# TensorE's queue in program order through the first part of a two-block kernel, with the lanes' products interleaved by hand

## The chip, the cores and the metric

One Trainium2 chip, one of its cores. The metric is device time in microseconds (us) of one execution. Engines: TensorE (PE; its weight loads are PEld), VectorE (DVE), ScalarE (ACT), GpSimd (POOL), SyncE (SP). "q" behind an engine's name is its queue of DMA issues.

## What is computed

All in float32, 256 tokens of width 1024. The first block takes x through two attention layers and a final norm. The second block takes that x (256 tokens) and a context ctx (256 tokens) through two layers. A layer normalises both with a modulation from a conditioning vector, forms q, k, v, pool, convolution and gate projections, attends, merges three branches, and then applies a feed-forward part with 16384 experts of which each token chooses 16 in each of 8 heads:

```python
q = (xc @ w_q).reshape(PEER_CHUNK, PEER_HEADS, 2, PEER_HALF)
s = jnp.einsum('thid,hikd->thik', q, sub_keys)
s1, i1 = lax.top_k(s[:, :, 0], PEER_TOPK); s2, i2 = lax.top_k(s[:, :, 1], PEER_TOPK)
...
top_s, pos = lax.top_k(cand, PEER_TOPK)
gate = jax.nn.softmax(top_s, axis=-1)
hid = jax.nn.gelu(jnp.einsum('td,thkd->thk', xc, u_emb[eidx]))
return jnp.einsum('thk,thkd->td', gate * hid, v_emb[eidx])
```

In the last layer only x goes on; ctx gives keys and values.

## The kernel before

**Products.** A weight chunk is 128 x 1024 (512 KB). `WS` (L253) loads chunks on a DMA queue and splits each into a high part (ScalarE, L281) and a rest (VectorE, L282), `LEAD` = 2 chunks ahead; `mm3` (L405, L409 to L411) makes 24 matmuls of a chunk, three for each of 8 pieces. A chunk that is not split ("whole") goes through `mm1` (L416): 8 products in whole precision, each recorded as two matmuls. All SBUF tiles of 4 KB a partition share one pool of 42 pages ("pg"): chunks, splits, activations, gathered rows, tables. PSUM has 3 banks for products ("u") and 5 for all small work ("m").

**Who sets the order.** The program is a set of Python generators that record instructions; `lead`, `par` and `along` interleave them by the costs that they yield ("units"). `lead(main, (side, r))` advances the side until it has r units for each unit of the main lane; `par` advances whichever has the least share of its own weight; `along(main, side, rate)` takes one step of the side for each 1/rate units. The order in which the generators record is the program order. The context runs with a timeline simulation: each engine's queue is then filled by a scheduler that takes, at each moment of its simulated time, the first instruction in program order that is ready. On the chip each queue runs in the order so fixed.

**Stages.** (1) The x lane: the first block (`b1`, L693) and then layer 0's mixer for x. Beside it, at rate 2.0, the ctx lane: ctx's mixer, then ctx's choice of experts (`choose`) with layer 1's modulation. ctx's 256 tokens x 128 experts are computed by row operations (`rows`): each gathers one 128 x 1024 tile through POOL's queue (L1381) and takes one VectorE instruction (L1392, a dot product, or L1401, an accumulation). They start when ctx's lane is done, 0.32 for each unit of x's lane. (2) Layer 0's choice for x (`ffn_start`): `topk` makes 16 whole chunks of products and, for each head, four key scores (L1241) in one "m" bank, from which VectorE selects (L1248 to L1253); after heads 3 and 7 it combines (to L1309). The first `SOLO` = 24 steps run alone. Then `gbuild`: for 8 blocks of 32 tokens and 4 parts each, VectorE makes two one-hot operands (L1487, L1489), TensorE multiplies them (L1495), ScalarE evicts (L1499), and ScalarE's queue stores a block as 4 DMAs to a table G in DRAM (L1504). Beside it, at weights 100 and 20 x 3.41, `peer` makes the hidden products of the first 20 of 128 expert chunks, 16 of them whole. (3) The dense product (`peer`): for each of 128 expert chunks, the hidden product if not made yet, its weighting by G (loaded at L1548, L1551 to L1554) and 12 matmuls of 512 columns into four accumulators (L1578 to L1580). Row operations run along at 0.25 (choice) and 0.45 (dense product) for each unit. (4) Layer 1: mixer, choice, dense product.

**The norm.** `rms_bcast` (L464): squares on ScalarE (L472), a matmul with ones (L474), an eviction (L476), a second matmul (L479), thirteen small VectorE steps (L396 to L403), two diagonals (L498), and a matmul that spreads them over the partitions (L501). Before, nothing is yielded inside. `attn_causal` and `attn2` run a head in three steps: scores and softmax (`first`), transposes (`second`, one unit behind; L656, L1015), the product with v (`third`).

Of the kernel before, what the change touches and what calls it, by code (L numbers as in the profile page):

```python
# [34 lines left out]
NPRE = (16, 20), (20, 28)  # L35
# [257 lines left out]
class Ker:  # L293
# [170 lines left out]
    def rms_bcast(s, hch, n):  # L464

        nc = s.nc
        st = s.ps("m")
        if n == 8:

            for g in range(0, n, 4):  # L470
                sq = s.pg([128, 4, T], F32, "sq")
                nc.scalar.activation(sq, hch(g, 4), AF.Square)  # L472
                for k in range(4):
                    nc.tensor.matmul(st[32 * k:32 * k + 32, :T], s.ones[:, 0:32], sq[:, k], start=g == 0, stop=g == 4)  # L474
            gs = s.s1([128, T], "gs")
            nc.scalar.copy(gs, st[:, :T])  # L476
            ss = s.ps("m")
# [4 lines left out]
        else:  # L482
            for g in range(0, n, 4):
                m = min(4, n - g)
                sq = s.pg([128, 4, T], F32, "sq")
                nc.scalar.activation(sq[:, :m], hch(g, m), AF.Square)
                for k in range(m):
# [16 lines left out]
    def rms(s, h, n=8):  # L504
        rbs = s.s1([128, T], "rbs")
        s.nc.vector.tensor_copy(rbs, s.rms_bcast(lambda g, m: h.t[g // 4][:, :], n))
        return rbs

    def norm_hl(s, h, a, b, name, n=8, rbs=None):

        nc = s.nc
        rbs = rbs if rbs is not None else s.rms(h, n)
        o = HL(s, name, n)
        for k in range(n):
# [6 lines left out]
            else:  # L521
                nc.scalar.activation(oh, y, AF.Identity, bias=b(k))
                nc.vector.scalar_tensor_tensor(ol, y, b(k), oh, op0=OP.add, op1=OP.subtract)
        return o

    def norm_f(s, h, a, b, o):

        nc = s.nc
        rbs = s.rms(h)
        for k in range(8):  # L530
            y = s.s1([128, T], "ny")
            nc.vector.scalar_tensor_tensor(y, h.ch(k), a(k), rbs, op0=OP.mult, op1=OP.mult)
            nc.scalar.activation(o.ch(k), y, AF.Identity, bias=b(k))  # L533
        return o
# [88 lines left out]
    def attn_causal(s, scores, bias, init, scale, val, emit):  # L623
# [49 lines left out]
        for i in range(18):  # L673
            if i < 16:
                first(i)
            if 1 <= i < 17:
                second(i - 1)
            if i >= 2 and i % 2 == 1:
                third((i - 3) // 2)
            yield 1.7  # L680
# [12 lines left out]
    def b1(s, x, eng, out):  # L693
# [8 lines left out]
        hn = s.norm_hl(x, lambda k: s.V("norm_w", k), None, "hn")  # L702
        del x
        ws.load(W1)
        yield 1.0
# [81 lines left out]
        hn = s.norm_hl(x, lambda k: s.V("norm_w", 8 + k), None, "hn")  # L787
# [48 lines left out]
        cqn = s.norm_hl(cq, lambda k: s.V("cqn", k), None, "cqn", 2)  # L836
        ckn = s.norm_hl(ckv, lambda k: s.V("ckvn", k), None, "ckn", 1)
# [49 lines left out]
        rb = s.rms_bcast(lambda g, m: x.t[g // 4][:, :], 8)  # L887
# [7 lines left out]
    def rows_hl(s, rr, lo, n):  # L895
# [12 lines left out]
        nc.vector.tensor_tensor(rl[z], tb[z, :T], rh[z], op=OP.subtract)  # L908
        return rh[z], rl[z]


    def qkv(s, l, hn, ws, rope, want_q, r):
# [26 lines left out]
        for a, off, _ in todo:  # L939
            for hf in range(2):  # L940
                sq = s.pg([128, 4, T], F32, "sq")
                nc.scalar.activation(sq, a.t[hf], AF.Square)
                for k in range(4):
# [9 lines left out]
        rh, rl = s.rows_hl(rr, 0, 16)  # L953
        yield 8.0
# [29 lines left out]
    def attn2(s, l, q, kv, sr, o):  # L984
# [45 lines left out]
        for i in range(18):  # L1030
            if i < 16:
                first(i)
            if 1 <= i < 17:
                second(i - 1)
            if i >= 2:
                third(i - 2)
            yield 3.0

        bank = s.ps("m")
        for hf in range(2):  # L1040
            sq = s.pg([128, 4, T], F32, "sq")
            nc.scalar.activation(sq, o.t[hf], AF.Square)
            for k in range(4):
# [6 lines left out]
        rh, rl = s.rows_hl(rr, 64, 8)  # L1050
        yield 4.0
# [108 lines left out]
    def mixer(s, l, st, src, ws, eng, res, kvx, late=None, before=None, seq=False, h=None, rbs=None, side=None):  # L1160
# [7 lines left out]
        hn = s.norm_hl(h, lambda k: s.a1[l][:, k, st:st + 1], m0, "hn", rbs=rbs)  # L1168
# [50 lines left out]
        res["xn"] = s.norm_f(h, lambda k: s.a2[l][:, k, st:st + 1], s.mod(l, st, 3), Act(s, F32, "xn"))  # L1219
# [3 lines left out]
    def topk(s, l, xn, ws, eng, res, rows=False):  # L1223
# [8 lines left out]
        for h, sb in s.lin(ws, xn, 16):  # L1232
            if sb is None:
                yield 2.6
                continue
            qf = s.s2([128, 512], "qf")
            nc.scalar.copy(qf, sb)
# [17 lines left out]
            if h % 4 < 3:  # L1255
                continue
# [38 lines left out]
            for j in range(2):  # L1295
                for hf in range(2):
# [13 lines left out]
                    yield TY  # L1310
        ts = tp[:, 2].rearrange("p h t k -> p (h t) k")
# [158 lines left out]
    def gbuild(s, res, G, eng, ntc=8):  # L1470
# [7 lines left out]
        iob = io[:, None, :, :].to_broadcast(sh)  # L1478
# [289 lines left out]
```

## Time and profile before

| | us |
|---|---|
| median of 3 runs | 3698.21 |
| lowest, highest | 3693.96, 3700.71 |
| the profiled execution | 3691.09 |
| its span, first to last instruction | 3689.3 |
| busy in the span: PE, PEld, DVE | 3258.1, 2966.9, 2790.7 |
| ACT, POOL | 1485.0, 935.6 |
| moved by DMA | 941.10 MB, mean 255 GB/s |

A timeline row gives start, length, engine, line, operation, output <- inputs, count, and in brackets the idle time of the engine before it with what ended it. A wait row gives the waiting engine and line, the releaser, and the total, the number and the longest of the waits. A granted clock of 1.00 is TensorE's upper level (2.4 GHz), 0.50 the lower (1.2 GHz); in between is a mean over the stretch.

### The profile page before, as it was taken

Reading aid. Unit: us, or ns where it says so; the run is one execution under the profiler, and the core shown is the slowest. Engines: PE = TensorE matmul, PEld = TensorE weight load, DVE = VectorE, ACT = ScalarE, POOL = GpSimd, SP = SyncE. Lnnn points to the kernel's source line nnn. Section 1 sums busy time; section 2 is a strip of 40 time slices with the busy share of each in tenths; the row PEclk is TensorE's granted clock in tenths of the full one; section 3 lists DMA queues with packets and bytes.
Section 4 is the critical chain, followed back from the end, with each engine's and each line's share of the span. In section 5 each row is a group of like instructions: output and inputs, shape, how many; then the busy total and the mean of one; then the engine's idle time right before and its main releaser. Section 6 shows DMA issues by size and latency. Waiting matters only on the chain. (4 is left out here: it accounts for less than half of the span.)

```text
span 3689.3 us, 61049 instructions
## 1 busy us (share of the span) xinstructions
PE 3258.1 (88%) x23324; PEld 2966.9 (80%) x23324; DVE 2790.7 (76%) x5722; ACT 1485.0 (40%) x2785; POOL 935.6 (25%) x831
## 2 busy tenths in 40 slices
PE   6989989996799885679999999778998689999999
PEld 5976889766689774668888888767988589999999
DVE  4356585578899889799989999788465978777655
ACT  3444345323355313333443444333353154444443
POOL 2002101212343512365555555232000003111000
PEclk9989999998899897889999999888999899999999
DMA  8536446756688845999999999776525089888764
GB/s 298 160 126 215 146 138 189 274 183 225 238 299 280 321 161 181 344 408 386 384 379 386 379 387 381 248 280 231 158 88 192 12 262 354 307 285 286 263 217 153
DMA packets 315430, 941.10 MB, mean 255 GB/s; under 512 B 29616, under 2 KB 93136, under 8 KB 315136
## 3 DMA queue, kind: packets, MB, share of 16 engines
q1 hardware_dynamic: 130848, 468.77, 35.7%
q0 software_dynamic: 118816, 432.76, 32.3%
q10 hardware_dynamic: 65472, 35.66, 3.2%
q8 instruction: 183, 3.00, 0.3%
q14 instruction: 111, 0.91, 0.1%
HBM read 893.01 MB, written 43.02 MB: 254 GB/s over the span
## 5 line engine op out<-in xcount | busy, mean ns | idle before, releaser
L282 DVE TENSOR_TENSOR wb<-wr,wa 128x1024 fp32r<-128x1024 f32 x846 | 1015.4, 1222 | 321.5 <-ACT wa L281 304.9
L281 ACT CAST wa<-wr 128x1024 fp32r<-128x1024 f32 x846 | 856.3, 1046 | 108.3 <-DMA wr<-in_w 39.0
L409 PE MATMUL pu<-hnh,wa 128*128 128x256 f32 x2000 | 586.0, 293 | 47.9 <-ACT wa L281 45.9
L411 PE MATMUL pu<-hnh,wb 128*128 128x256 f32 x2000 | 583.4, 293 | 17.1 <-DVE wb L282 17.0
L410 PE MATMUL pu<-hnl,wa 128*128 128x256 f32 x2000 | 578.5, 290 | 0.0
L409 PE MATMUL pu<-xh,wa 128*128 128x256 f32 (+1 forms) x1760 | 492.1, 280 | 10.1 <-ACT wa L281 9.6
L1381 POOL DMA_INDIRECT row<-in_pu,ridx x256 | 365.1, 1426 | 520.7 <-DVE wb L282 124.5
L410 PE MATMUL pu<-xl,wa 128*128 128x256 f32 (+1 forms) x1760 | 491.2, 279 | 0.9 <-DVE xl L1538 0.9
L411 PE MATMUL pu<-xh,wb 128*128 128x256 f32 (+1 forms) x1760 | 491.4, 279 | 0.0
L1381 POOL DMA_INDIRECT row<-in_pv,ridx x256 | 354.4, 1384 | 473.5 <-DVE wb L282 133.0
L409 PEld LDWEIGHTS pu<-hnh,wa 128*128 128x128 f32 x2000 | 397.7, 199 | 65.0 <-ACT wa L281 52.0
L411 PEld LDWEIGHTS pu<-hnh,wb 128*128 128x128 f32 x2000 | 395.8, 198 | 32.5 <-DVE wb L282 21.9
L410 PEld LDWEIGHTS pu<-hnl,wa 128*128 128x128 f32 x2000 | 397.4, 199 | 3.9 <-issue 3.5
L409 PEld LDWEIGHTS pu<-xh,wa 128*128 128x128 f32 x1760 | 338.5, 192 | 20.1 <-ACT wa L281 14.5
L410 PEld LDWEIGHTS pu<-xl,wa 128*128 128x128 f32 x1760 | 338.5, 192 | 4.6 <-DVE xl L1538 1.1
L411 PEld LDWEIGHTS pu<-xh,wb 128*128 128x128 f32 x1760 | 338.5, 192 | 1.8 <-issue 0.4
L1401 DVE SCALAR_TENSOR_TENSOR racc<-row,rwg,racc 128x1024 f32<-128x1024 f32 x254 | 325.5, 1282 | 0.4
L416 PE MATMUL pu<-xn,wr 128*128 128x256 f32 (+1 forms) x1344 | 311.9, 389 | 4.7 <-ACT xn L533 4.7
L1392 DVE CUSTOM_DVE_ANT_0 row<-row,xr 128x1024 f32<-128x1024 f32 x256 | 311.2, 1221 | 0.0
L1528 ACT ACTIVATE gel<-pu 128x256 f32<-128x256 f32 (+1 forms) x208 | 77.2, 371 | 577.8 <-PE pu L411 553.0
L416 PEld LDWEIGHTS pu<-xn,wr 128*128 128x128 f32 x1344 | 261.6, 199 | 41.7 <-issue 6.2
L1570 PE MATMUL pm<-W,wa 128*128 128x224 f32 x1024 | 276.1, 275 | 1.6 <-ACT wa L281 1.6
(427 smaller groups left out, 6487.7 us busy)
## 6 DMA issues: line engine op xcount, KB each, us to landing
wr<-in_w SPq DMA_DIRECT2D x288, 512.0 KB
wr<-in_pu SPq DMA_DIRECT2D x256, 512.0 KB
wr<-in_pv SPq DMA_DIRECT2D x256, 512.0 KB
wr<-in_w POOLq DMA_DIRECT2D x130, 512.0 KB
wm<-in_wmod POOLq DMA_DIRECT2D x96, 512.0 KB
G<-gt ACTq DMA_DIRECT2D x60, 512.0 KB
gp<-G SPq DMA_DIRECT2D x32, 512.0 KB
gp<-G SPq DMA_DIRECT2D x32, 448.0 KB
```

The lines of the kernel that those rows point to most:

```text
L281: nc.scalar.copy(a, r)
L282: nc.vector.tensor_tensor(b, r, a, op=OP.subtract)
L409: mm(out, ah, bh, start=i == 0, stop=False)
L410: mm(out, ah, bl, start=False, stop=False)
L411: mm(out, al, bh, start=False, stop=i == n - 1)
L416: s.nc.tensor.matmul(out, w[:, k * 128:(k + 1) * 128], x(k), start=k == 0, stop=k == 7)
L1381: nc.gpsimd.indirect_dma_start(out=t, out_offset=None, in_=tab[w], in_offset=bass.IndirectOffsetOnAxis(ap=s.ridx[:, tt, i:i + 1], axis=0))
L1392: v.tensor_tensor_reduce(t, t, xr[tt], 1.0, 0.0, OP.mult, OP.add, hid[:, i:i + 1])
L1401: v.scalar_tensor_tensor(out[tt], t, wg[:, i:i + 1], out[tt], op0=OP.mult, op1=OP.add)
L1528: nc.scalar.activation(g, bank[:, :NT], AF.Gelu_apprx_tanh)
L1570: mm(o, vh[:, c], W[:, 0], start=j == 0 and d % 2 == 0, stop=False, skip_group_check=True)
```

## The change

A block `manual_schedule` for TensorE alone is put around everything up to and with layer 0's `ffn_start`: in it TensorE's queue is the program order, and the scheduler still orders the other engines. From the dense product on it orders TensorE too, as before. The program order is changed to go with it: the norms, the q/k norm and the row splits become generators with yields between their steps; `attn_causal` and `attn2` run `second` two units behind, in 19 steps of 1.6 and 2.85 units instead of 18 of 1.7 and 3.0 (in `attn_causal` `third` moves by one unit too); `topk` records the selection of a head after the products of the next one, `gbuild` the table products of a part after the operands of the next part (layer 1's `gbuild` and its `topk` for x keep the old order: `skew=False`); the first norm of ctx runs in turn with the first norm of `b1`; and the hidden products ahead of the dense product become 24, 20 of them whole. They are interleaved at 6.0 units for each unit of the rest of `topk`, then with `gbuild` at weights 50 and 64.

```diff
-NPRE = (16, 20), (20, 28)
+NPRE = (20, 24), (20, 28)
+EARLY = 6.0, 50.0
...
                 nc.scalar.activation(sq, hch(g, 4), AF.Square)
+                yield 1.5
                 for k in range(4):
                     nc.tensor.matmul(st[32 * k:32 * k + 32, :T], s.ones[:, 0:32], sq[:, k], start=g == 0, stop=g == 4)
             gs = s.s1([128, T], "gs")
             nc.scalar.copy(gs, st[:, :T])
+            yield 1.0
...
             nc.vector.tensor_scalar(dg[:, tt], s.C("ident"), r[:, tt:tt + 1], None, op0=OP.mult)
+        yield 4.0
         rb = s.ps("m")
...
-        for i in range(18):
+        for i in range(19):
             if i < 16:
                 first(i)
-            if 1 <= i < 17:
-                second(i - 1)
-            if i >= 2:
-                third(i - 2)
-            yield 3.0
+            if 2 <= i < 18:
+                second(i - 2)
+            if i >= 3:
+                third(i - 3)
+            yield 2.85
...
+        prev = None
+        for h, sb in s.lin(ws, xn, 16):
+            if sb is None:
+                yield 2.6
+                continue
+            qf = s.s2([128, 512], "qf")
+            nc.scalar.copy(qf, sb)
+            if not skew:
+                yield from select(h, qf)
+                continue
+            if prev is not None:
+                yield from select(*prev)
+            prev = h, qf
+        if skew:
+            yield 2.6
+            yield from select(*prev)
...
-def ffn_start(k, l, rx, ws, G, pe, tot, *more, ntc=8):
+def ffn_start(k, l, rx, ws, G, pe, early, tot, ntc=8):
     eng = k.nc.gpsimd
-    tk = k.topk(l, rx["xn"], ws, eng, rx)
+    tk = k.topk(l, rx["xn"], ws, eng, rx, skew=bool(early))
     for i in range(SOLO):
         yield next(tk, None)
-    yield from par(k, (chain(tk, lambda: k.gbuild(rx, G, k.nc.scalar, ntc)), TG), (until(pe), tot), *more)
+    pre = until(pe)
+    if not early:
+        gb = lambda: k.gbuild(rx, G, k.nc.scalar, ntc, skew=False)
+        yield from par(k, (chain(tk, gb), TG), (pre, tot))
+        return
+    yield from lead(tk, (pre, early))
+    yield from par(k, (k.gbuild(rx, G, k.nc.scalar, ntc), 64.0), (pre, tot))
...
+    with k.tc.manual_schedule(engines={mybir.EngineType.PE}):
...
+        def norm_ctx():
+            rbc.append((yield from k.rms(hc[0])))
+        drain(par(k, (until(b1), 1.0), (norm_ctx(), 1.0)))
...
+        drain(along(ffn_start(k, 0, rx, ws, k.G[0], pe, *EARLY), rows, RATE[2]))
     rx.clear()
     drain(along(pe, rows, RATE[3]))
```

## Rows read from the trace of the kernel before

**Rows 1.** Stretches: length, busy PE, PEld, DVE, ACT, POOL, PEclk, DMA share, GB/s.
```profile
0.00:1292.00 1292.00, 1141.31 (x8018) 1001.26 (x8019) 887.25 (x2193) 523.43 (x921) 297.51 (x363) 0.92 0.64 221
1292.00:1410.00 118.00, 75.35 (x371) 66.21 (x370) 101.53 (x524) 10.41 (x23) 9.82 (x8) 0.82 0.33 123
1410.00:1532.00 122.00, 93.15 (x726) 78.95 (x724) 111.73 (x172) 53.92 (x275) 35.91 (x27) 0.86 0.88 289
...
1560.00:1640.00 80.00, 61.23 (x211) 46.01 (x212) 80.00 (x114) 26.88 (x41) 50.52 (x39) 0.83 1.00 400
1640.00:2300.00 660.00, 612.49 (x3798) 549.56 (x3797) 605.38 (x798) 272.80 (x425) 361.00 (x245) 0.98 0.99 385
2300.00:3689.00 1389.00, 1258.13 (x10088) 1209.00 (x10087) 990.38 (x1907) 589.17 (x1085) 169.86 (x142) 0.94 0.66 223
```

**Rows 2.** Waits of TensorE from 0 to 1310 us: total, times, longest.
```profile
PE pm L501 <- DVE dg L498: 28.8, 7, 10.1
PE pm L474 <- ACT sq L472: 18.8, 6, 6.5
...
PE pm L656 <- DVE p L649: 10.4, 4, 3.9
```

**Rows 3.** Slices of 20 us, columns as in rows 1.
```profile
0.00:20.00 20.00, 4.37 (x24) 2.26 (x24) 7.13 (x30) 5.72 (x9) 8.79 (x20) 1.00 0.91 334
...
260.00:280.00 20.00, 15.37 (x60) 12.88 (x61) 7.47 (x40) 4.52 (x16) 0.00 (x0) 0.50 0.03 11
...
600.00:620.00 20.00, 20.00 (x169) 20.00 (x169) 13.67 (x15) 9.52 (x11) 2.64 (x5) 1.00 0.65 207
...
840.00:860.00 20.00, 5.09 (x27) 3.01 (x28) 18.42 (x80) 2.49 (x3) 3.53 (x4) 0.50 0.46 165
...
960.00:980.00 20.00, 7.15 (x31) 6.14 (x32) 17.36 (x37) 0.36 (x1) 2.33 (x2) 0.50 0.44 166
...
1080.00:1100.00 20.00, 20.00 (x148) 17.98 (x148) 19.97 (x39) 8.31 (x15) 10.14 (x7) 1.00 0.84 273
```

**Rows 4.** Timeline of TensorE at the end of the selection.
```profile
1358.21 7.07 PE L416 MATMUL pu<-xn,wr 128*128 128x256 f32 x32
1369.10 1.16 PE L1241 MATMUL pm<-keyT,qf 128*128 128x128 f32 x8 [3.81 <-ACT qf L1237]
1402.29 0.47 PE L1344 MATMUL pm<-ct,tt 128*128 128x128 f32 x1 [32.03 <-ACT tt L1343]
1409.56 1.33 PE L1344 MATMUL pm<-ct,tt 128*128 128x128 f32 x5 [6.80 <-ACT tt L1343]
...
1416.01 4.66 PE L416 MATMUL pu<-xn,wr 128*128 128x256 f32 x16
```

**Rows 5.** Timeline of SyncE's queue, 1300 to 1370 us.
```profile
1302.89 62.46 SPq L268 DMA_DIRECT2D wr<-in_pu  x6
```

**Rows 6.** Waits of SyncE's queue, 1300 to 1640 us: total, times, longest.
```profile
SPq L268 <- DMA G<-gt: 109.3, 14, 23.1
SPq L268 <- DVE top L1309: 43.8, 1, 43.8
```

**Rows 7.** Timeline of VectorE: the selection's end, the tables' begin and end.
```profile
1408.73 0.45 DVE L1309 TENSOR_TENSOR top<-eq 128x64 f32<-128x64 f16 x2
...
1411.16 1.29 DVE L1487 TENSOR_TENSOR hot<-io,id 128x1024 f16<-128x1024 f16 x2
...
1520.08 1.28 DVE L1489 TENSOR_TENSOR gat<-hot,id 128x1024 f16<-128x1024 f16 x2
```

**Rows 8.** Timelines of ScalarE's queue and of VectorE, from tables to dense product.
```profile
1533.00 10.08 ACTq L1504 DMA_DIRECT2D G<-gt  x3
...
1556.31 1.42 DVE L1551 TENSOR_TENSOR gpre<-gpre,gp 128x256 f32<-128x256 f32 x4
```

**Rows 9.** The page's costliest groups: row operations on VectorE (busy, mean ns, idle before).
```profile
L1401 DVE SCALAR_TENSOR_TENSOR racc<-row,rwg,racc 128x1024 f32<-128x1024 f32 x254 | 325.5, 1282 | 0.4
...
L1392 DVE CUSTOM_DVE_ANT_0 row<-row,xr 128x1024 f32<-128x1024 f32 x256 | 311.2, 1221 | 0.0
```

More of the change, by code (lines that the diff above doesn't have):

```diff
@@ L511, in norm_hl @@
         nc = s.nc
-        rbs = rbs if rbs is not None else s.rms(h, n)
+        if rbs is None:
+            rbs = yield from s.rms(h, n)
         o = HL(s, name, n)
@@ L528, in norm_f @@
         nc = s.nc
-        rbs = s.rms(h)
+        rbs = yield from s.rms(h)
         for k in range(8):
@@ L1028, in third @@
             nc.scalar.copy(o.ch(h)[:, qt * 128:(qt + 1) * 128], bank[:, :128])
-        for i in range(18):
+        for i in range(19):
             if i < 16:
                 first(i)
-            if 1 <= i < 17:
-                second(i - 1)
-            if i >= 2:
-                third(i - 2)
-            yield 3.0
+            if 2 <= i < 18:
+                second(i - 2)
+            if i >= 3:
+                third(i - 3)
+            yield 2.85
         bank = s.ps("m")
@@ L1049, in attn2 @@
         z = slice(64, 72)
[L1050 to L1051 removed]
+        yield 3.0
+        rh, rl = yield from s.rows_hl(rr, 64, 8)
         for i in range(4):
@@ L1478, in gbuild, with tables @@
         iob = io[:, None, :, :].to_broadcast(sh)
+        def tables(hot, gat, gt, tc, q):
+            for u in range(2):
+                bank = s.ps("m")
+                for i in range(4):
+                    t = u * 4 + i
+                    for j in range(2):
+                        mm(bank[:, i * 128:(i + 1) * 128], hot[:, 0, t // 2, :, t % 2], gat[:, j, t // 2, :, t % 2],
+                           start=j == 0, stop=j == 1)
+                for jq in range(4):
+                    o = q * 8 + u * 4
+                    nc.scalar.activation(gt[jq][:, :, o:o + 4],
+                                         bank.rearrange("p (t j) -> p j t", t=4)[:, jq * 32:(jq + 1) * 32, :],
+                                         AF.Copy, scale=1.0 / GS)
+                yield 1.0
+            if q < 3:
+                return
+            for jq in range(4):
+                eng.dma_start(G[jq * 8:(jq + 1) * 8, :, tc].rearrange("g p j t -> p g (j t)"),
+                              gt[jq].rearrange("p (g j) t -> p g (j t)", g=8))
+        prev = None
         for tc in range(ntc):
@@ L1489, in gbuild @@
                     v.tensor_tensor(gat[:, j], hot[:, 1], w[2 + j], op=OP.mult)
[L1490 to L1505 removed]
+                if not skew:
+                    yield from tables(hot, gat, gt, tc, q)
+                    continue
+                if prev is not None:
+                    yield from tables(*prev)
+                prev = hot, gat, gt, tc, q
+        if skew:
+            yield from tables(*prev)
     def peer(s, l, xn, G, eng, eng2, nnat, npre, out, keep=None, NT=T, rows=None):
@@ L1718, in program @@
-    rows = k.rows(cn, acc)
-    ws = WS(k, ai["w2"][0], sy, whole=WHOLE)
-    ctx = chain(k.mixer(0, 1, ctx0, wc, gp, rc, lambda: [], md, seq=True, h=hc.pop(), rbs=rbc.pop()),
-                lambda: par(k, (choose(), 69.0), (k.mods(1, gp), 26.0)))
-    xs = chain(b1, lambda: k.mixer(0, 0, k.hd["x"], ws, sy, rx, lambda: [k.kv_load(sy)], seq=SEQ, h=x3.pop()))
-    drain(lead(xs, (chain(ctx, lambda: scaled(rows, RATE[0] / RATE[1])), RATE[0]), (k.setup2(), 0.5)))
-    kp = {}
-    pe = k.peer(0, rx["xn"], k.G[0], sy, sy, *NPRE[0], k.hd["x"], kp)
```

107 lines of the change are left out of this document (50 added, 57 removed).

## The prediction

> **What bounds the kernel now.** I read the table of stretches first [rows 1]. It shows a kernel with several regimes. From 0 to 1292 us two lanes (the token lane x, the context lane ctx) share TensorE, which is busy for 1141 of 1292 us: TensorE is the nearest thing to a bound, with 151 us idle. From 1292 to 1532 us (layer 0's choice) VectorE is busy 213 of 240 us and bounds. From 1560 to 2300 us (the dense product) the DMA share is 0.99 to 1.00: the DMA engines bound. The change touches the queue order of the first two and, through what is moved ahead, the third.
>
> Second, the waits of TensorE up to 1310 us [rows 2], to see what its idle time hangs on: the norm chains lead (28.8 us for the diagonal, 18.8 us for the squares), and attention's transposes add 10.4 us. Third, single slices of 20 us [rows 3]: a full slice of split products holds 169 matmuls, 0.118 us each, so a chunk of 24 costs 2.8 us; the slices at 260, 840 and 960 us hold 60, 27 and 31, at a granted clock of 0.50 (the 1.2 GHz level). These are latency holes, not work.
>
> Fourth, the end of the choice. TensorE finishes the last key scores at 1370 us and then stands at one head, the transpose of the chosen indices, for 32.0 and 6.8 us [rows 4]. Six weight chunks for the dense product had been issued by 1366 us [rows 5], but the next chunk product, at 1416, stands behind that head. VectorE works through: its last selection step is at 1408.7, the table building starts at 1411.2, the last table operand ends at 1521.4 [rows 7]. Then a serial chain: the last table store occupies ScalarE's queue to 1543, and the first weighted activation comes at 1556.3 [rows 8].
>
> **The change part by part.** The sum is made against the profiled execution, 3691 us (span 3689.3); the median of the runs shown is 7 us above it.
>
> *Program order with fill in the norm chains.* The new yields (1.5, 1, 4 and 2 units in each norm) put the other lane's products between a norm's steps. Of the 47.6 us in the two norm rows, much lies in the first 20 us, where TensorE idles 15.6 us [rows 3] because both lanes are only starting and nothing can fill. The layer-1 norm of x, its two small latent norms and the ctx norm have the ctx or x lane beside them; the waits there are small and I take -10. At 835 to 865 us stands x's final norm: here ctx is at its end and there is no product to fill with, but there VectorE is busy 18.4 of 20 us with ctx's selection [rows 3]. In units of the yields ctx ended at 226 of x's 223 up to that norm's end (452 units at rate 2.0); with the change it ends at 237 of 255 (473 at 2.0), 18 units earlier, so the norm meets row operations but no selection: -8. Bounds: 0 and -47.6.
>
> *Attention one step further apart.* The second step now trails by two units instead of one. The first lane's transposes wait 10.4 us in all [rows 2]; I take half, -5; bounds 0 and -10.4. The step count grows from 18 to 19 with smaller units, so the lanes' pace hardly changes.
>
> *Rows taken earlier.* Since ctx ends earlier and x's lane has 58 more units, x's lane yields (622-237) x 0.32 = 123 row operations before the choice instead of (564-226) x 0.32 = 108. The choice's units fall from 187 to 165, at 0.25 that is 41 operations instead of 47. A row operation costs 1.22 or 1.28 us on VectorE [rows 9] and one gather of 512 KB on POOL's queue. So 15 x 1.25 = 19 us of VectorE are added ahead of 1292 us, where VectorE is busy 20.0 of 20 us in the busiest slices, as at 1080 us [rows 3], though 887 of 1292 on the whole [rows 1]; I take half, +10, bounds 0 and +19. Six fewer in the choice, where VectorE bounds, is -7. About ten fewer are left for layer 1's mixer; between 0 and -12 there, and since VectorE is at 990 of 1389 us after 2300, I take -3.
>
> *The choice.* The selection of a head now follows the next head's products. That is worth at most the delay of the first selection by one pair of whole-precision chunks, 7.1 us [rows 4], and after the first head VectorE's backlog covers it; the scheduler was free to order it so before, so I take 0, bounds 0 and +7. Eleven chunk products (36 units at 6.0 times the six left in the selection, 3.41 units each) go into the 39 us hole: a whole-precision chunk is half of 7.07 us [rows 4], 3.5, and 11 make 39 us. That hole is not on the path, which is VectorE's; the work is moved, and its worth is only that the last four products no longer stand between the tables and the dense product. But they ran beside the store chain of [rows 8], which stays. So for this I take -4; bounds 0 and -28, the whole stretch from 1532 to 1560.
>
> *Four more chunks ahead.* In the dense product a step without its own hidden product holds 12 matmuls, one with it 36. The cost of the two kinds is 80 us x 12/211 = 4.55 us and 660 x 36/3798 = 6.26 us [rows 1]. Four steps change kind: 4 x 1.71 = -7. By bytes, 4 x 0.524 MB at 385 GB/s is -5.4, the near bound. The four chunks that are no longer split cost TensorE 3.5 instead of 2.8 us each, under VectorE's work, and take four splits off ScalarE and VectorE; I count nothing for it.
>
> Sum: -10 -8 -5 +10 -7 -3 -4 -7 = -34, so 3657 for a profiled execution and 3664 at the level of the median. **Forecast: 3660 us.**
>
> A rule on how to read this weighs in. What the rows show: the slice at 1080 us is 20.0 of 20 us busy with 148 matmuls, where 169 fit; weight loads are busy 1001 us of the first 1292, 291 us short, against 151 us by matmul time [rows 1, 3]. The Trainium skill (Perfetto Trace Analysis, "Identifying the Most-Contended Engine") says matmul busy time hides headroom and LDWEIGHTS busy time is the measure. By that, the part to be filled is 291/151 = 1.9 times as large and the sum would be lower; it is a rival below.
>
> **The rivals.** *Head of the queue blocked (slower).* While ctx chooses, 680 to 870 us, each score product needs a free PSUM bank, and banks come free only as VectorE selects; there are five for all small work. In the old order the scheduler could put x's products ahead; in program order x's attention and output product stand behind a score product that waits. The last part of a selection takes VectorE 39 us (1370 to 1409) [rows 4, 7], and there are two such parts in ctx's choice. Price: up to 2 x 39 = 78 us, with the -5 of attention lost and the rest of the sum kept: 3664 + 5 + 78 = 3747 at most, 3708 if half of it shows. It decides once VectorE's backlog exceeds one pair of chunks, about 7 us. For it: [rows 4], where a blocked head held loaded work for 32 us, and VectorE's 18.4 of 20 us at 840. Against: there is a pair of chunks of distance between products and selection. The Trainium skill (TensorE: Matmul & The Clock Gate, "Step-by-step: what each phase is for") says that matmuls stay in program order and only weight loads are pulled ahead; the trace agrees, by the 32.0 us above.
>
> *The early products come late (no change; the change doesn't do what it says).* A chunk load needs a free page of the 42. In the old trace SyncE's queue waited 43.8 us for a page last used by the selection and 109.3 us behind table stores [rows 6]. If the eleven loads wait like that, in fixed order their 39 us stand ahead of the first tables, and the tables start up to 39 us late; with pages for VectorE to run ahead some 10 us of it are hidden. Price +29: 3693. For: those waits. Against: six loads were issued by 1366 in the old trace, and gather pages come free all the time.
>
> *The first part has more slack than matmul time shows (faster still).* If the new order fills 1.9 times as much of the norm and attention waits, -23 becomes -44: 3643.
>
> **How the numbers follow.** A measurement of this kernel can tell about 0.2%, 7 us, from no change. Chances: forecast 0.52 (its own range 3630 to 3688), more slack 0.14, early products late 0.12, blocked head 0.22. The late case straddles no change: 0.02 of it goes to faster. So faster 0.68, same 0.10, slower 0.22. The range reaches down to 3605, which takes the 32 us of the norm rows that can be filled (47.6 - 15.6) and half of the store chain, and up to 3735, most of the blocked-head case.
>
> **What would show it.** Right: a chunk product in the stretch after the last key score instead of a 32 us gap; granted clock above 0.50 there; the waits for the diagonal under 20 us up to the choice; first weighted activation some 25 us or more ahead of 1556; dense steps with 12 matmuls for 24 steps instead of 20. Wrong: waits of TensorE in the key-score or attention lines of several us each between 680 and 870 (the blocked head); SyncE waits of tens of us before the early chunk loads with tables starting after 1440 (late products); a choice that starts later than 1292 us, which would say that the first part lost by program order whatever the choice gained.

## The result and the profile after

| | before | after |
|---|---|---|
| median of 4 runs, us | 3697.47 | 3636.77 |
| lowest, highest | 3693.96, 3700.71 | 3632.30, 3645.06 |
| span of the profiled execution | 3689.3 | 3634.8 |

The ratio is 0.9839, 95% interval 0.9819 to 0.9858: faster by 1.6%. The forecast of 3660 stood 23 us too high, and its range holds the result. To see where the 54.5 us between the two profiled executions went, I read five moments from each trace: the first key score of layer 0's choice for x, the first weighting of an expert chunk (the first in the dense product), the start of the dense product's last matmul, the last product of layer 1's mixer, and the end.

| stretch | before | after | difference |
|---|---|---|---|
| start to layer 0's choice | 1307.5 | 1289.2 | -18.3 |
| choice to first weighting | 248.8 | 245.2 | -3.6 |
| dense product | 762.5 | 754.7 | -7.8 |
| layer 1's mixer | 507.4 | 482.5 | -24.9 |
| the rest | 863.1 | 863.2 | +0.1 |

The largest share lies in layer 1's mixer, which the forecast had all but left out. The stretches after, as in [rows 1] (length, busy PE, PEld, DVE, ACT, POOL, granted clock, DMA share, GB/s):

```profile
0.00:1274.00 1274.00, 1123.78 (x8018) 989.65 (x8019) 900.87 (x2214) 524.28 (x918) 307.57 (x378) 0.92 0.66 230
1534.00:2290.00 756.00, 679.46 (x4015) 598.63 (x4016) 699.42 (x935) 305.09 (x475) 426.49 (x291) 0.97 0.99 389
```

The first row is cut where as many matmuls are done as in the first of [rows 1], 8018, and is 18 us shorter. Yet TensorE is idle for 150 us in it, as before (151). What shrank is its busy time, 1141 to 1124 us for the same number of matmuls: the busy time of the records holds more than work. The second row is still bound by DMA, 0.99 of the engines.

The waits of TensorE from 0 to 1310 us (waiting line, releaser, total, times, longest), as in [rows 2]:

```profile
PE pm L478 <- ACT sq L475: 24.4, 6, 9.6
PE pm L508 <- DVE dg L504: 21.3, 5, 6.5
...
PE pm L915 <- DVE rr L405: 14.4, 1, 14.4
...
PE pm L913 <- DVE rr L405: 12.6, 1, 12.6
PE pm L666 <- DVE p L659: 7.8, 3, 4.2
```

The norms' two waits sum to 45.7 us, where they were 47.6: the fill inside the norms hardly shows here. The transposes of the x lane's attention fell from 10.4 to 7.8. The q/k norm (L913 and L915, before the change L903 and L905, whose rows stand with the run e2_manual_only below) waits longer, 27.0 us instead of 15.0. So the named waits don't say where the first part got faster. A stretch does; the first row below is of the kernel before, the second of the changed one (columns as above):

```profile
250.00:500.00 250.00, 234.31 (x1606) 194.98 (x1606) 148.85 (x399) 101.88 (x211) 35.17 (x68) 0.90 0.52 174
250.00:500.00 250.00, 244.55 (x1841) 215.94 (x1842) 158.33 (x396) 109.53 (x202) 39.70 (x75) 0.95 0.56 187
```

In these 250 us, which hold the x lane's first attention, the changed kernel gets through 235 matmuls more, though TensorE is busy only 10 us longer. By kind, they are 261 split products more, 31 us at 0.118 us each, and 26 other matmuls fewer. Part of that lead is given back where x's final norm and, right behind it, the first norm of layer 0's mixer stand, from 800 to 840 us (same columns; what answers to it before is the slice at 840 in [rows 3]):

```profile
800.00:820.00 20.00, 4.30 (x28) 2.45 (x27) 15.10 (x38) 1.43 (x2) 16.34 (x13) 0.57 0.92 326
820.00:840.00 20.00, 5.16 (x26) 2.75 (x26) 16.64 (x52) 6.92 (x13) 5.19 (x5) 0.50 0.94 349
```

Two slices are nearly empty of matmuls instead of one. At the end of the selection the hole of 32.0 us of [rows 4] is filled, as TensorE's timeline shows (start, length, line, operation, count, idle time before it):

```profile
1356.06 2.08 PE L1250 MATMUL pm<-keyT,qf 128*128 128x128 f32 x8 [4.23 <-ACT qf L1327]
1357.93 31.91 PE L418 MATMUL pu<-xn,wr 128*128 128x256 f32 x144
1389.67 0.27 PE L1371 MATMUL pm<-ct,tt 128*128 128x128 f32 x1
1391.62 1.39 PE L1371 MATMUL pm<-ct,tt 128*128 128x128 f32 x5 [1.67 <-ACT tt L1370]
1392.85 8.76 PE L418 MATMUL pu<-xn,wr 128*128 128x256 f32 x32
1401.44 0.62 PE L1512 MATMUL pm<-gat,hot 128*128 128x128 f16 x8
```

144 matmuls in whole precision are nine chunks, 3.5 us each; the clock is at its upper level there (0.98 from 1358 to 1392, where it was 0.50 in the hole). What stands between the tables and the dense product, as in [rows 8] (ScalarE's queue, then VectorE):

```profile
1521.51 4.31 ACTq L1523 DMA_DIRECT2D G<-gt  x3
```

```profile
1534.39 1.43 DVE L1591 TENSOR_TENSOR gpre<-gpre,gp 128x256 f32<-128x256 f32 x4 [8.10 <-DMA gp<-G]
```

The store chain is over 17 us earlier, and the first weighting 21.9 us earlier. In layer 1's mixer I compare the waits of TensorE from the last product of the dense part to the mixer's end, before:

```profile
PE pu L409 <- ACT wa L281: 30.6, 4, 12.3
PE pm L501 <- DVE dg L498: 9.2, 2, 6.4
PE pm L1015 <- DVE nb L1002: 5.7, 2, 2.8
...
PE pm L474 <- ACT sq L472: 5.3, 4, 2.4
...
PE pm L1015 <- DVE p L1008: 4.5, 2, 4.3
```

and after:

```profile
PE pu L411 <- ACT wa L283: 28.3, 4, 8.6
PE pm L508 <- DVE dg L504: 6.4, 1, 6.4
...
PE pm L478 <- ACT sq L475: 2.7, 2, 2.4
```

The transposes of `attn2` waited 10.2 us for the softmax; that wait is gone. The norms wait 5.4 us less. Both functions are shared with layer 0, so their new spacing works here too, outside the block with the fixed queue. The mixer also holds ten row operations fewer, 49 instead of 59.

### The profile page after: what moved, and what is told of

It is laid out like the page before. It is cut to its first block, busy times and chain, and to the rows that moved or that the text cites. A ratio compares the mean times of both kernels' runs of the same rounds, so it can differ in the third digit from the quotient of the medians.

```text
span 3634.8 us, 60941 instructions
## 1 busy us (share of the span) xinstructions
PE 3238.1 (89%) x23292; PEld 2955.7 (81%) x23292; DVE 2781.1 (77%) x5718; ACT 1482.8 (41%) x2779; POOL 945.3 (26%) x831
## 3 DMA queue, kind: packets, MB, share of 16 engines
q1 hardware_dynamic: 130848, 468.77, 36.3%
## 5 line engine op out<-in xcount | busy, mean ns | idle before, releaser
L1408 POOL DMA_INDIRECT row<-in_pv,ridx x256 | 369.9, 1445 | 473.5 <-DVE wb L284 110.6
L411 PE MATMUL pu<-xh,wa 128*128 128x256 f32 (+1 forms) x1728 | 484.3, 280 | 1.0 <-ACT xh L1577 1.0
L412 PE MATMUL pu<-xl,wa 128*128 128x256 f32 (+1 forms) x1728 | 483.6, 280 | 1.5 <-DVE xl L1578 1.5
L413 PE MATMUL pu<-xh,wb 128*128 128x256 f32 (+1 forms) x1728 | 482.7, 279 | 0.0
L411 PEld LDWEIGHTS pu<-xh,wa 128*128 128x128 f32 x1728 | 333.3, 193 | 10.4 <-ACT wa L283 4.4
L418 PE MATMUL pu<-xn,wr 128*128 128x256 f32 (+1 forms) x1408 | 324.0, 388 | 3.2 <-ACT xn L542 3.2
L418 PEld LDWEIGHTS pu<-xn,wr 128*128 128x128 f32 x1408 | 274.0, 199 | 45.0 <-issue 10.0
```

Of the source, the lines that this page charges most:

```text
L411: mm(out, ah, bh, start=i == 0, stop=False)
L412: mm(out, ah, bl, start=False, stop=False)
L413: mm(out, al, bh, start=False, stop=i == n - 1)
L418: s.nc.tensor.matmul(out, w[:, k * 128:(k + 1) * 128], x(k), start=k == 0, stop=k == 7)
L1408: nc.gpsimd.indirect_dma_start(out=t, out_offset=None, in_=tab[w], in_offset=bass.IndirectOffsetOnAxis(ap=s.ridx[:, tt, i:i + 1], axis=0))
```

## The experiments

The changed kernel does several things, and the forecast's rivals say that the queue order itself decides. Each run below undoes one part or does one alone. Ratios are to the kernel before, timed beside each run; "x's choice at" is the moment of the first row of the table above. Differences between two runs in us are the difference of the ratios times 3692 (about what the kernel before took beside them).

How far two executions of one order differ can be read from two of these runs. In e11_layer1_early TensorE, GpSimd and SyncE run the same instructions in the same order as in the changed kernel up to layer 1's choice, and VectorE and ScalarE do but for a few neighbours that change places; yet x's choice begins 4.7 us later and layer 1's choice 9.6 us later. In e10_no_early, where the order is the same up to the last key scores, x's choice begins 5.7 us later. So a difference of 5 us in a stretch of two traces, or of 10 us at the end, tells nothing by itself.

**The fixed queue taken away (e1_no_manual).** The changed program, with the scheduler ordering TensorE all the way:

```diff
-    with k.tc.manual_schedule(engines={mybir.EngineType.PE}):
+    if True:
```

> The changed kernel's program, but the scheduler orders TensorE's queue all the way, as before. Theory 'rows and order': the part of the gain that comes from row operations taken earlier (some 25 us, seen in layer 1's mixer) and from four more chunks ahead (8 us) needs no fixed queue and stays; the choice's start goes back from 1289 to about 1300-1308 us; total 3645 to 3665, that is 10 to 25 us slower than the changed kernel. Rival 'the fixed queue is all of it': back to 3690 or more. Rival 'the rewriting of the program is all of it': 3632 to 3642, no difference.

Measured: 3636.56 us, 0.9854 (0.9837 to 0.9870). The interval overlaps that of the changed kernel: no difference can be told. The gain is in the rewritten program order. The scheduler takes the first ready instruction in program order, and so carries much of that order to the chip: of the 8016 matmuls ahead of x's choice, half stand within 3 places of where the fixed queue has them, and 97% within 72 (three split chunks). x's choice began 9.6 us earlier (1279.6; in e12_no_early_sched, which has the same queue up to there, 1282.5, and in three runs with the fixed queue 1289.2 to 1294.9), but the last product of the dense part started at the same time (2289.0 and 2289.1). One place where the fixed queue loses time ahead of the choice is the q/k norm, which waits 27.0 us in the changed kernel and 12.8 us here, in the same window:

```profile
PE pm L915 <- DVE rr L405: 12.2, 1, 12.2
...
PE pm L913 <- DVE rr L405: 0.6, 1, 0.6
```

**The fixed queue alone (e2_manual_only).** The kernel before with the block put around the same region, and nothing else:

```diff
+    with k.tc.manual_schedule(engines={mybir.EngineType.PE}):
...
+        drain(along(ffn_start(k, 0, rx, ws, k.G[0], pe, NPRE[0][1] * 3.41), rows, RATE[2]))
```

> The old program with TensorE's queue in program order over the same part, and nothing else changed. Theory: without products recorded between the steps of the norms, of attention and of the choice, TensorE stands at each of those heads; the head that stood for 32 us at the end of the selection is joined by one at every head's key scores (8 in each choice, about 5 us each, 80 us) and by the attention steps (2 x 16 + 32 units, 1 to 2 us each): 3750 to 3850. Rival 'a fixed order is good in itself': 3640 to 3690.

Measured: 3718.27 us, 1.0069 (1.0053 to 1.0086). Slower by some 26 us, so the old program order was not fit for a fixed queue, though by less than expected. x's choice begins 27 us late by its first key score, 34 us by its first product. (The trace is of the longest of the runs, 3732.9 us, 15 us above the median.) Where: the waits of TensorE up to 1330 us,

```profile
PE pm L501 <- DVE dg L498: 36.8, 9, 10.4
PE pm L905 <- DVE rr L403: 20.0, 2, 13.9
PE pm L1015 <- DVE p L1008: 19.4, 9, 3.4
...
PE pm L903 <- DVE rr L403: 11.2, 2, 8.7
...
PE pm L1241 <- ACT qf L1237: 5.6, 8, 0.7
```

and, in the kernel before, up to 1310 us (the norm's 28.8 us are in [rows 2]):

```profile
PE pm L905 <- DVE rr L403: 12.4, 1, 12.4
...
PE pm L903 <- DVE rr L403: 2.6, 1, 2.6
...
PE pm L1015 <- DVE p L1008: 2.3, 3, 1.6
```

Not the key scores of ctx's choice (5.6 us in 8 waits) but the norm, the q/k norm and the attention transposes one unit behind the softmax hold the queue.

**Attention back at one unit, in the fixed queue (e6_no_attn_skew).**

```diff
-        for i in range(19):
+        for i in range(18):
...
-            if 2 <= i < 18:
-                second(i - 2)
+            if 1 <= i < 17:
+                second(i - 1)
```

(`third` and the units likewise, in both functions.)

> The changed kernel (fixed queue) with both attentions back at one unit between softmax and transposes, 18 steps. Theory: in a fixed queue every transpose then stands until VectorE has divided, 16 heads in each of four attentions, 0.5 to 1 us each: 32 to 64 us lost: 3665 to 3700. Rival 'there is always a product of the other lane or branch between': 3632 to 3650.

Measured: 3681.51 us, 0.9967 (0.9953 to 0.9982): 47 us of the gain are lost. x's choice begins at 1321.0 instead of 1289.2. The waits of the transposes up to 1280 us show it (in the changed kernel they are 7.8 and 0.9 us):

```profile
PE pm L666 <- DVE p L659: 20.6, 8, 5.1
...
PE pm L1028 <- DVE p L1021: 19.1, 8, 3.5
```

**The same, with the scheduler all the way (e7_no_attn_skew_sched).** The edit above together with that of e1.

> The same edit with the scheduler all the way. Theory 'units': the scheduler finds the filling by itself, and the distance in the program matters little: within 8 us of e1, 3629 to 3645. Rival 'attention one step further apart': 20 to 40 us lost: 3657 to 3677.

Measured: 3684.69 us, 0.9983 (0.9967 to 0.9999), 48 us above the run without the fixed queue. So the distance is not worth its 47 us because the queue is fixed; the scheduler gains as much from it. x's choice begins at 1316.9 instead of 1279.6. The named waits of the transposes are 22.3 us here (12.7 and 9.6), and the stretch from 250 to 500 us holds 1667 matmuls where the run without the fixed queue has 1771.

**Attention's distance alone (e8_before_skew),** in the kernel before (the same lines, the other way).

> The kernel before with only the attention steps moved one unit further apart, the scheduler all the way. Theory 'units': 0 to 10 us gained: 3682 to 3692. Rival 'attention one step further apart': 20 to 40 us gained: 3652 to 3672.

Measured: 3671.44 us, 0.9943 (0.9927 to 0.9960): -21 us from this edit alone. x's choice begins 11 us earlier, and layer 1's mixer takes 496.4 instead of 507.4 us: there the waits at L1015 fell from 10.2 to 2.4 us, and nothing else of its waits moved by more than 1 us:

```profile
PE pu L409 <- ACT wa L281: 30.6, 4, 12.3
PE pm L501 <- DVE dg L498: 9.2, 2, 6.4
...
PE pm L474 <- ACT sq L472: 5.3, 4, 2.4
...
PE pm L1015 <- DVE p L1008: 1.4, 1, 1.4
...
PE pm L1015 <- DVE nb L1002: 1.0, 1, 1.0
```

What the edit changes is the pace of a lane in attention. The 48 transposes of the x lane's first attention (shortest, median and longest in ns, then the first and the last start in us) in the kernel before, in this run and in the changed kernel:

```profile
L656 PE MATMUL pm<-ct,p x48: 270/273/475, 266.2 to 373.4; 128*128 128x128 f32 x48
L656 PE MATMUL pm<-ct,p x48: 272/273/477, 266.3 to 352.7; 128*128 128x128 f32 x48
L666 PE MATMUL pm<-ct,p x48: 272/273/478, 250.0 to 330.5; 128*128 128x128 f32 x48
```

From the first to the last it is 107 us, 86 us with this edit alone, and 80 us; in e7 it is 90 us where the run without the fixed queue has 84.

**No yields in the norms (e5_no_norm_yields),** scheduler all the way, with the row rate set so that as many row operations as in e1 come before x's first key score (127 and 128):

```diff
-RATE = 2.0, 0.32, 0.25, 0.45, 0.3, 2.0
+RATE = 2.0, 0.358, 0.25, 0.45, 0.3, 2.0
...
-        yield 4.0
+        yield 0.0
```

(and the other yields of the norm likewise.)

> The rewritten program with the scheduler all the way (as in e1), but the yields inside the norms set to 0, so that a norm is recorded in one piece again; the row rate is set so that 123 row operations still lie before the choice. Theory 'units': the yields work through what they do to the program order, that is to the scheduler's priorities: ctx's lane runs ahead of x's and finds room in x's norms, in layer 1's mixer too; without them 15 to 35 us are lost against e1: 3650 to 3672. Rival 'attention one step further apart' does it: within 8 us of e1, 3629 to 3645.

Measured: 3647.39 us, 0.9873 (0.9856 to 0.9889), 7 us above the run without the fixed queue, the two intervals overlapping. So by the ratios no difference can be told. In the traces x's choice begins 19.6 us later (1299.2), and the last product of the dense part starts 12.9 us later (2301.9): the yields are worth some 13 us by the traces, if anything.

**Row operations: as few as before, in the changed kernel (e3_rows_back).** 113 instead of 128 before x's first key score.

```diff
-RATE = 2.0, 0.32, 0.25, 0.45, 0.3, 2.0
+RATE = 2.0, 0.281, 0.25, 0.45, 0.3, 2.0
```

> The changed kernel with the row operations' rate in the first part lowered from 0.32 to 0.281, so that about 108 instead of 123 lie before the choice, as before the change; the rest is left for layer 1's mixer. Theory 'rows': the first part gains 0 to 10 us (15 fewer VectorE steps of 1.25 us), layer 1's mixer loses about 18 (as many steps, each alone on its path): total 3640 to 3655, 5 to 15 us slower. Rival 'layer 1's 25 us come from what the scheduler happened to do': layer 1 unchanged within 5 us, total 3627 to 3637.

Measured: 3642.42 us, 0.9866 (0.9850 to 0.9883), 10 us above the changed kernel by ratio, 4 by the profiled executions, and the intervals overlap. x's choice begins no earlier (1292.2), and layer 1's mixer takes 7.4 us longer (489.9), which is hardly more than two executions of one order differ by. So no difference can be told.

**Row operations: as many as after, in the kernel before (e4_before_rows)** (the rate 0.364; 129 instead of 114 before x's first key score).

> The kernel before with that rate raised from 0.32 to 0.364, so that about 123 row operations lie before the choice. Theory 'rows': layer 1's mixer gains 18 us, the first part loses 0 to 15: total 3675 to 3695, 2 to 22 us faster than before. Rival 'layer 1's gain is the scheduler's accident': 3697 to 3712, no gain and the cost in the first part alone.

Measured: 3680.41 us, 0.9970 (0.9959 to 0.9982), -11 us. x's choice begins 18.1 us later, close to the 19 us that 15 row operations cost VectorE, and layer 1's mixer is 21.8 us shorter (485.6). So here the rows are paid in full ahead of the choice and more than paid back in layer 1; in the changed kernel, no cost ahead of it shows. The dense product is 8.5 us shorter too (754.0 instead of 762.5), though it has no more chunks ahead than before; why was not followed.

**The old order inside the choice (e9_no_choice_skew),** with the fixed queue: a head's selection right behind its own products, and a part's table products right behind its own operands.

```diff
-    tk = k.topk(l, rx["xn"], ws, eng, rx, skew=bool(early))
+    tk = k.topk(l, rx["xn"], ws, eng, rx, skew=False)
...
-    yield from par(k, (k.gbuild(rx, G, k.nc.scalar, ntc), 64.0), (pre, tot))
+    yield from par(k, (k.gbuild(rx, G, k.nc.scalar, ntc, skew=False), 64.0), (pre, tot))
```

(ctx's `topk` too.)

> The changed kernel (fixed queue) with the selection of a head recorded right after that head's products again, in both choices, and the table products right after their own operands. Theory: in a fixed queue the key scores of each of 2 x 8 heads stand until ScalarE has copied the head's product, 1.5 to 4 us each, and each of 32 table groups until VectorE has its operand; in x's choice VectorE's work covers it, in ctx's the other lane loses it: 10 to 30 us lost against the changed kernel, 3643 to 3667. Rival 'VectorE covers both': within 8 us, 3627 to 3643.

Measured: 3649.44 us, 0.9884 (0.9867 to 0.9900): 17 us lost. The selection of x ends at the same time (1390.2 and 1391.2), but the tables take 144.2 us from there to the last operand instead of 127.7: each table product waits for the operand recorded just ahead of it.

```profile
PE pm L1512 <- DVE gat L1537: 29.7, 25, 3.3
```

The row is from 1385 to 1560 us. In the changed kernel, from 1360 to 1600 us:

```profile
PE pm L1618 <- ACT wa L283: 28.3, 4, 17.3
PE pm L1512 <- DVE gat L1537: 15.2, 15, 4.6
```

The half of the edit in ctx's choice costs nothing that shows: x's choice makes its first product at 1272.7 us, in the changed kernel at 1273.4.

**No early products (e10_no_early),** with the fixed queue: the 24 hidden products are no longer interleaved with the rest of the selection, but recorded beside the tables.

```diff
-EARLY = 6.0, 50.0
+EARLY = 1e-9, 92.0
```

> The changed kernel (fixed queue) with no chunk product in the end of the selection: all 24 beside the building of the tables, up to the same 85 per cent of it. Theory 'the hole is not on the path': the gap after the last key scores opens again, 25 us and more, and the first weighted activation moves by 0 to 10 us: 3633 to 3648. Rival 'filling the hole is a main part of the gain': 25 to 40 us lost: 3660 to 3675.

Measured: 3668.35 us, 0.9939 (0.9919 to 0.9958): 37 us lost. The selection ends 5.6 us later than in the changed kernel only because x's choice begins 5.7 us later; it takes as long without products in its hole as with them. The tables take 164.0 us from there instead of 127.7, 36.3 us more. Between the first and the last table product stand 19 whole chunks, where the changed kernel has 9: ten chunks of 3.5 us are 35 us. A view of TensorE inside the table building:

```profile
1505.41 1.54 PE L1512 MATMUL pm<-gat,hot 128*128 128x128 f16 x24
1511.51 0.45 PE L411 MATMUL pu<-xh,wa 128*128 128x256 f32 x1 [4.56 <-ACT xh L1577]
1517.21 0.58 PE L412 MATMUL pu<-xl,wa 128*128 128x256 f32 x1 [5.25 <-DVE xl L1578]
...
1522.13 0.63 PE L1512 MATMUL pm<-gat,hot 128*128 128x128 f16 x8
```

Here the first split chunk waits for the split of its activations, and the next table product starts 15 us after the last one ended. In the changed kernel split chunks stand between table products too, but wait only 2.5 us for that split.

**The same, with the scheduler all the way (e12_no_early_sched).** The edit above together with that of e1.

> The changed program without the early products (as in e10_no_early: the 24 hidden products are no longer interleaved with the rest of the selection, but recorded beside the table building), and with the scheduler ordering TensorE all the way (as in e1_no_manual). It completes a table of two by two: early or not, fixed queue or not. Theory A (the early products are worth their 37 us by what they take from between the tables, whoever orders the queue): about 3668, ratio 0.992 to 0.997, the table building (end of the selection to the last table operand) some 155 us or more. Theory B (the price in e10 belongs to the fixed queue, in which a chunk product that waits for its splits holds back the tables behind it; a scheduler takes the tables first): about 3637 to 3645, ratio 0.985 to 0.988, the table building about 130 us, as in the run with early products.

Measured: 3649.53 us, 0.9898 (0.9873 to 0.9924): 13 us by the medians (16 by ratio) above the run with the early products and no fixed queue, 6.5 by the profiled executions; the tables take 145.1 us, where that run has 129.5, and 17 whole chunks stand between table products instead of 8. The result lies between the two theories. Nine more chunks, 32 us of products, lengthen the tables by 16 us here, where ten lengthened them by 36 in the fixed queue. The early products are worth some 13 us of themselves, and over 20 more where the queue is fixed. That a scheduler puts table products ahead of a chunk that isn't ready would explain it; the waits for the activations' split, 3.5 us here and 9.8 there, point that way but are not the whole of it. Without the early products the fixed queue loses some 15 to 20 us against the scheduler (0.9939 against 0.9898; the intervals overlap by 0.0005); with them no cost can be told.

**A try to beat both: layer 1's choice done in the same manner (e11_layer1_early)** (fixed queue, early products, and 32 products ahead instead of 28).

```diff
-NPRE = (20, 24), (20, 28)
+NPRE = (20, 24), (20, 32)
...
-    drain(ffn_start(k, 1, rx, ws, k.G[1], pe, None, NPRE[1][1] * 2.99, ntc=TD // 32))
+    with k.tc.manual_schedule(engines={mybir.EngineType.PE}):
+        drain(ffn_start(k, 1, rx, ws, k.G[1], pe, 6.0, 55.0, ntc=TD // 32))
```

> The changed kernel with the same order given to layer 1's choice: skewed selection and tables, fixed queue, 32 instead of 28 chunk products ahead, at 6.0 units for each of the rest of the selection and then at weights 55 and 64. There TensorE is the bound of the dense product that follows (898 matmuls in each 100 us, clock 1.00), and it idles 30 us after the last key scores and makes 8 split chunks alone after the last table. Theory: a product moved into that gap is time gained: 15 to 28 us: 3608 to 3622. Rival 'the store chain of the tables is on the path in any case': 0 to 5 us: 3631 to 3637.

Measured: 3649.31 us, 0.9887 (0.9859 to 0.9916): slower than the changed kernel by 18 us by ratio, 13 by the profiled executions. Of the 13 us, 9.6 are there before layer 1's choice begins, where nothing was edited, so the edit itself costs 3.5 us in the traces, and that it costs anything is not shown. It does not gain what was expected. The hole in layer 1's selection is filled with 11 chunks, but from the choice's first product to the first weighted one it takes 249.0 instead of 234.7 us; the dense product behind it is 10.8 us shorter, with four more chunks ahead. TensorE's waits from 2895 to 3045 us are the table operands and, at the end, the first weighted product:

```profile
PE pm L1512 <- DVE gat L1537: 14.1, 10, 4.0
PE pm L1610 <- ACT wa L283: 12.9, 1, 12.9
```

Which of the three edits costs the 14 us was not taken apart. No run beat the changed kernel.

## Why the prediction was right or wrong

**Sign and range** held. The sum of -34 became -54.5 in the profiled pair; single steps were further off, and their errors partly cancelled: the attention and the early products were priced at -9 together, and each turned out to be worth more than 35 us in the fixed queue. That the total lies in the range is in part luck.

**Fill in the norms, -10, and x's final norm, -8.** Together -18 were taken; without the yields 13 us are lost by the traces and nothing that can be told by the ratios. The step on x's final norm failed: "ctx ends 18 units earlier, so the norm meets row operations but no selection". The order came so (ctx's selection ends at 796 us, before the norm, where it ended at 854, behind it), but not the gain of 8 us. The two waits of that norm and of the next one behind it are 23.3 us after (12.5 for the squares and 10.8 for the diagonals, in the slices at 800 and 820) and were 19.4 (5.1 and 14.3). ctx's products are no longer there as fill, and the row operations delay the norm in their turn. The longest wait, 9.6 us, goes back to the last addition to x (L791): its product ended at 800.5 us, but in VectorE's queue it stands behind four row operations that wait for their gathered rows:

```profile
801.62 1.23 DVE L1419 CUSTOM_DVE_ANT_0 row<-row,xr 128x1024 f32<-128x1024 f32 x1 [3.53 <-DMA row<-in_pu,ridx]
...
808.74 0.68 DVE L791 TENSOR_TENSOR x<-x,pu 128x512 f32<-128x512 f32 x1
```

**Attention, -5, bounds 0 and -10.4.** This is the term that was mis-sized most: -21 alone, -47 on top of the rest. Two things were wrong. The bound was the first lane's named wait, 10.4 us, as if a lane's delay cost only what is put down to the matmul that waits; in e7 the named waits of the transposes are 22.3 us, and the choice begins 37 us later than in e1. And the edit sits in functions that layer 1's mixer calls too: in e8 7.8 of 10.2 us of named waits go there, and 11 us of time. e8 shows both halves by themselves.

**Rows, +10 -7 -3.** The counts held: 14 row operations more before x's first key score (128 instead of 114; forecast 123 instead of 108), and ten fewer in layer 1's mixer. The price ahead of the choice is +18 in the kernel before, near the upper bound, and none that shows in the changed one; what they give back in layer 1's mixer is 21.8 us in the kernel before, beyond the bound of -12, and 7.4 in the changed one. The step that failed is "since VectorE is at 990 of 1389 us after 2300, I take -3": an average over layer 1, where the mixer is the stretch in which the rest of the rows runs. Through which wait they cost so much there was not settled: between before and after VectorE's time in the mixer falls by 13 us (357.7 to 344.4), and the waits for `wa` fall to 19.4 us in e4 but stay at 28.3 in the changed kernel.

**The choice's order, 0.** Refuted: 17 us. The step looked at the selection alone, where VectorE's backlog does cover it (the selection ends within 1 us). The gain is in the tables, whose half of the same edit was not priced.

**The early products, -4.** Refuted: 37 us in the fixed queue, some 13 with the scheduler. "That hole is not on the path, which is VectorE's" was true of the hole; what counts is that each product made there is one less between the table products, which are on the path (9 chunks between them, or 19). The bound of -28, taken from the stretch behind the tables, did not look at them.

**"The store chain of [rows 8] stays."** It shortened: from the last table operand to the first weighting it is 15.5 us instead of 34.9. It is as short (15.0 to 15.5) in the runs without early products. But the tables themselves are built in 127.7 us from the selection's end instead of 112.2, with 24 products ahead instead of 20 and a row operation now and then between. So the whole from choice to first weighting gained only 3.6.

**Four more chunks ahead, -7.** The dense product took 7.8 us less, but 763.1 us, no less than before, in the run without the fixed queue, which has the same four chunks and began 8.5 us earlier; both end at the same time. And it took 754.0 us in e4_before_rows, which has not got them. What the four chunks are worth was not isolated.

**The rivals.** The blocked head exists: 26 us for the fixed queue alone. Its place was wrong (norm, q/k norm and transposes, not ctx's key scores). The changed program order removes it from the transposes but not from the q/k norm, which waits 27.0 us in the fixed queue and 12.8 with the scheduler; the 9.6 us by which the choice begins later are made up by the end of the dense product, 2289 us in both, so the total doesn't show them. The late early products did not happen: SyncE issued 15 chunk loads from 1283 to 1358 us and the tables start at 1401. "More slack than matmul time shows" put the choice's start at -34 (-44 and the rows' +10) against the forecast's -13; it came to -18. In its reading it was right: idle time by matmul records stayed at 150 us while the part got 18 us shorter. By that the trace agrees with the Trainium skill (Perfetto Trace Analysis, "Identifying the Most-Contended Engine") that matmul busy time is not a good measure of headroom. Of the measure that it names beside, the busy time of weight loads, 284 of 1274 us are idle after and 291 of 1292 before: it hardly moved either, so the factor that I made of it was too large.

**The signs** that were named: the chunks behind the last key score came, as did the clock (0.98). The wait for the diagonal was to be under 20 us and is 21.3; the first weighting was to be 25 us earlier and is 21.9; 268 weighted matmuls run before the first split hidden chunk in the dense product where 220 did, four steps of 12 more, as forecast.

## What to carry to other kernels

In this kernel, where two lanes share one engine, the order in which the program is recorded mattered more than who turns it into a queue: one more unit between a softmax and the transposes that need it was worth 21 to 48 us of 3690, the fixed queue nothing that could be told. Before pricing an edit in a helper, list every stage that calls it; here nearly half of the gain came from a stage outside the block that the change is named after. Don't bound such a step by the one wait that names it (10.4 us here); look at how long the lane takes from its first transpose to its last (107 us, and 86 with the edit alone). Before reading a difference of two traces, find a pair of runs whose queues are the same up to some point and see how far they differ there. And test parts from both sides: the parts undone here sum to far more than the 60 us between the medians, so none has a price of its own.

## What was not expected of the hardware

Two stretches of 250 us with nearly the same busy share of TensorE (234 and 245 us) hold 1606 and 1841 matmuls, at a granted clock of 0.90 and 0.95. The split products that came in are 31 us of work, but busy time grew by 10 us only; so by this estimate some 20 of the 234 us were waits inside the records or the lower clock. Busy time of the matmul records is not an amount of work. And the dense product ended at 2289 us whether it began at 1525.9 (without the fixed queue) or at 1534.4 us, with the DMA engines 0.99 busy: a lead won ahead of it can be lost in it. The earlier one, in columns as above:

```profile
1525.90:2289.00 763.10, 689.73 (x4008) 606.86 (x4009) 698.28 (x933) 304.12 (x474) 417.05 (x290) 0.95 0.99 384
```
